# A dense two-layer stage: input forms made earlier, the mixer's output product in one pass, and the first group's input order changed

## The chip, the core and the metric

One core of one Trainium2 chip runs the whole program in one launch. The metric is the device time of that launch in microseconds; lower is better.

## What is computed

The reference has two blocks over 512 tokens of width 1024, in float32. The first (a gated linear recurrence and a mixture of 32 experts) is not touched by the change. The second, `second_block`, has two layers, and each layer is three residual steps:

```
h = rmsnorm(x, g_ffn1); x = x + 0.5 * swiglu(h, w1_a, w3_a, w2_a)
h = rmsnorm(x, g_mix);  p = h @ w_in
x = x + (gate0 * y_f + gate1 * y_c + gate2 * y_p) @ w_o
h = rmsnorm(x, g_ffn2); x = x + 0.5 * swiglu(h, w1_b, w3_b, w2_b)
```

`swiglu(h)` is `(silu(h @ w1) * (h @ w3)) @ w2` with an inner width of 2816. `rmsnorm` divides each token by the root of the mean of its squares over all 1024 inputs. A last `rmsnorm` ends the program.

## The kernel before

**Numbers.** Every product is made in float32 by three matmuls (`mm3`, line 231): both operands are split into a rounded part (`hi`, written by ScalarE) and a remainder (`lo`, by VectorE), and hi x hi, hi x lo and lo x hi are added up in PSUM.

**Weights.** The class `Stream` loads weights as blocks of 128 x 2048 in a fixed order and cuts each in two halves of 128 x 1024. `_split` (lines 185 and 186) writes a half's rounded part `whi` on ScalarE and its remainder `wlo` on VectorE; there are 5 buffers of each. `advance(h)` splits until four halves lie ahead of half h. It is called in the program wherever a half has been used up, so its place in the text is its place in the queues of ScalarE and VectorE. Weights of `group` come in sets of seven halves with four sums among them; two sums are added by DMAs on POOL's queue (line 149, `accum_op`), two by VectorE (line 191). Ordinary loads stand on SP's queue (line 151). A block's slot is free again when its halves are split.

**X.** The residual is held as eight tiles X[0] to X[7] of 128 inputs by 512 tokens. Outputs are produced in the order JO = 0, 4, 1, 5, 2, 6, 3, 7.

**Feed-forward.** `ffn` (line 1526) goes through the inner width in three chunks CH (6, 8 and 8 tiles of 128). For each pair of inner tiles `group` (line 1458) computes w1 and w3 products with seven block products instead of eight (a Strassen-like scheme on 256-column halves); its inputs are sums and differences of pairs of X tiles, made by `forms(q)` (line 1339) from the tiles X[q] and X[q+4] scaled by the gain. `step(i, n, ps)` is one of the seven: 4 pairs q x 2 halves m x 3 matmuls of 256 columns, 24 in all, on the input form XS[n, q]. Step 0 uses n = 4 and step 1 uses n = 6. Between the steps ScalarE copies a PSUM bank on (`pv` is the copy of `pm`, line 1482), `after` runs leftovers of the group before and calls `advance`. In the very first chunk of the first layer (`std`) the plain scheme is used. There are 41 groups. The chunk's inner tiles then go through `out_part` (line 1405), whose order `out_order` starts the first two outputs without their last two inputs; each output, 24 matmuls of 512 columns with 8 inputs, is added to X[j] by `done` on VectorE (line 1571).

**What stands between two stages.** In a stage's last output product `done` also calls `nxt(j)`. Before a stage that uses `group` at once this is `prep_s` (line 1364): `gained` scales X[j] by the gain (ScalarE, 1337), `square` squares it (ScalarE, 1316) and adds the squares to `ssum` (POOL, 1319), and once both tiles of a pair are there `forms` is due. Both the sum and `forms` are not run at once but put in the list `late`, which the next `square` (after its own ScalarE instruction) or the end of the product empties by `flush`. In `forms` the lines that matter are 1346 (ScalarE, the rounded copy for n = 1 and 4), 1349 to 1351 (VectorE, sums), 1352, 1353 and 1356 (ScalarE, rounded copies), 1354 and 1357 to 1359 (VectorE, remainders). `rstd_1` (matmuls of `ssum` with ones, a root, Newton steps) and `rstd_2` (transposes into the row R) turn the sum of squares into the norm's factor; products in `group` are multiplied by R on their way out of PSUM. With `rstd` true, in the first group of a stage, `rstd_1` follows step 1 and `rstd_2` follows step 2.

**Mixer.** `mixer` (line 1576) makes eight gated tiles M[0] to M[7]. It does so in two halves of four; after each half `out_part2` (line 1432) adds that half's part of the product with w_o to all eight tiles of X, in a pipeline: the fourth input of an output is multiplied three outputs later (LAG2 = 3), and so the last three outputs all end within the last nine matmuls. Before the second half's product the mixer's buffers are closed and those of the next feed-forward (`open_ffn`, load slots `rawf` and `rawg` among them) opened. Three stages begin with a `group` on fresh forms: the second feed-forward of each layer, behind the mixer, and the first feed-forward of the second layer.

**Buffers.** Split inputs, forms, inner tiles and M share 45 slots `s` of 128 x 512; a feed-forward has 5 scratch tiles `t` and 2 wide ones `T`. PSUM has six banks `mm` and two `sv`.

Of the kernel before, what the change touches and what calls it, by code (L numbers as in the profile page):

```python
# [33 lines left out]
JO = (0, 4, 1, 5, 2, 6, 3, 7)  # L34
L2 = 2
NT_F = 5
LAG2 = 3
ALPHA = float(np.float32(2 ** 0.25))
LN_EPS = 1e-5
EPS = 1e-6  # L40
# [1202 lines left out]
def dense_phase(K):  # L1243
# [11 lines left out]
    def bank():  # L1255
        return pp.tile([128, 512], F32, name="mm", tag="mm", bufs=6)

    def sbank():

        return pp.tile([128, 512], F32, name="sv", tag="sv", bufs=2)  # L1260
# [49 lines left out]
    def flush():  # L1310
        while late:
            late.pop(0)()

    def square(k, E=nc.gpsimd):
        t = ssum if k == 0 else tmp()
        act(t, X[k], AF.Square)
        flush()
        if k:
            late.append(lambda: E.tensor_tensor(ssum, ssum, t, op=OP.add))

    def prep(k, g, sq=True):
        hi, lo = slot(), slot()
# [8 lines left out]
    def halves(t):  # L1331
        return t.rearrange("p (a b) -> p a b", a=2)
# [30 lines left out]

    def prep_s(k, g):
        gained(k, g)
        square(k)
        if k >= 4:
            late.insert(0, lambda: forms(k - 4))

    def rstd_1():  # L1370

# [33 lines left out]
    def out_part(x, done, tail=None):  # L1405

        nonlocal h
        n = 0
        ps = {}
        for j, ks in out_order(len(x)):  # L1410
            if tail and j == KD - 1:
                flush()
                tail(x, [tuple(t[:, q % 8 * 128:q % 8 * 128 + 128] for t in st.get(h + q // 8))
                         for q in range(n, n + len(x))])
                n += len(x)
                break
            if j not in ps:
                ps[j] = bank()
            for k in ks:
                w = st.get(h + n // 8)  # L1420
                sl = slice((n % 8) * 128, (n % 8 + 1) * 128)
                mm3(nc, ps[j], (w[0][:, sl], w[1][:, sl]), x[k], k == 0, k == len(x) - 1)
                n += 1
                if n % 8 == 0:
                    st.advance(h + n // 8 - 1)
            if ks[-1] == len(x) - 1:
                done(j, ps[j])
        flush()
        assert n % 8 == 0
        h += n // 8  # L1430

    def out_part2(x, done):

        nonlocal h
        ps = {}
        n = 0
        for i in range(KD + LAG2):
            for j, ks in ((i, range(3)), (i - LAG2, (3,))):
                if not 0 <= j < KD:
                    continue  # L1440
                if ks[0] == 0:
                    ps[j] = bank()
                for k in ks:
                    w = st.get(h + n // 8)
                    sl = slice((n % 8) * 128, (n % 8 + 1) * 128)
                    mm3(nc, ps[j], (w[0][:, sl], w[1][:, sl]), x[k], k == 0, k == 3)
                    n += 1
                    if n % 8 == 0 and n < 4 * KD:
                        st.advance(h + n // 8 - 1)
                if ks[0] == 3:  # L1450
                    done(JO[j], ps[j])
        flush()
        st.advance(h + 3)
        h += n // 8

    RB = [R[:, None, i * 256:(i + 1) * 256].to_broadcast([128, 2, 256]) for i in range(2)]
# [1 line left out]
    def group(hid, todo, rstd):  # L1458
# [1 line left out]

        nonlocal h

        def step(i, n, ps, first=False):
            w = st.get(h + i)
            for q in range(4):
                for m in range(2):
                    sl = slice(m * 512 + q * 128, m * 512 + (q + 1) * 128)
                    mm3(nc, ps[:, m * 256:(m + 1) * 256], (w[0][:, sl], w[1][:, sl]), XS[n, q],
                        first and q == 0 and m == 0, q == 3, True)

        def after(i, *fs):
            for f in todo[i:i + 1] + list(fs):
                f()
            st.advance(h + i)
# [1 line left out]
        def tile():  # L1476
            return wide().rearrange("p (t m b) -> p t m b", t=2, m=2)

        pm = bank()
        step(0, 4, pm, True)  # L1480
        pv = sbank()
        act(pv, pm, AF.Copy)
        after(0)
        pz = bank()
        step(1, 6, pz, True)
        zs = tmp()
        act(zs, pz, AF.Copy)
        if rstd:
            rstd_1()
        after(1)  # L1490
        step(2, 0, pv)
        pw = sbank()
        act(pw, pv, AF.Copy)
        after(2)
        if rstd:
            pr, = rstd_2(0)
            act(R, pr, AF.Copy)
        step(3, 2, pm)
        a = tile()
        after(3, lambda: STT(a[:, 1], halves(pm), -1.0, RB[1], op0=OP.mult, op1=OP.mult))  # L1500
        step(4, 1, pw)
        vs = tmp()
        act(vs, pw, AF.Copy)
# [72 lines left out]
    def mixer(l, nxt):  # L1576
# [105 lines left out]
        for g in range(4):  # L1682
# [7 lines left out]
            TT(f[:, 1:256], p1[:, 1:256], q[:, 1:256], op=OP.subtract)  # L1690
            TT(f[:, 511:256:-1], p1[:, 1:256], q[:, 1:256], op=OP.add)
            FT.append(hilo(f))
        for half in range(2):
            M = []
            for j in range(4 * half, 4 * half + 4):
                g = j // 2
                gc, gf = gate(), gate()
                w = st.get(h)
                py, pf, pq = sbank(), bank(), sbank()
                chunk(w, BC, py)  # L1700
                mm3(nc, pf, (w[0][:, 512:640], w[1][:, 512:640]), FT[g], True, True)
                mm3(nc, pq, (w[0][:, 640:768], w[1][:, 640:768]), PL[g], True, True)
                st.advance(h)
                h += 1
                TT(gc, gc, py, op=OP.mult)
                TT(gf, gf, pf, op=OP.mult)
                TT(gc, gc, gf, op=OP.add)
                gp = gate()
                STT(gp, pq, vc("pscale", KD * l + j), gp, op0=OP.mult, op1=OP.mult)
                TT(gc, gc, gp, op=OP.add)  # L1710
                M.append(hilo(gc))
                if j % 2 == 0 and g < 3:
                    PL[g + 1] = pool(g + 1)

            def done(j, ps):
                TT(X[j], ps, X[j], op=OP.add)
                if half == 1:
                    nxt(j)
            if half == 1:
                close()  # L1720
                open_ffn(2 * l + 1)
            out_part2(M, done)

    def last(k):
        square(k)
# [95 lines left out]
def layout(I):  # L1821
# [70 lines left out]
    for l in range(L2):  # L1892
# [27 lines left out]
        for j in range(KD):  # L1920
            g, r = divmod(j, 2)
            sl = slice(128 * r, 128 * r + 128)
            misc = np.zeros((128, 8, 128), f)
            misc[:, 0:4] = tco[j]
            misc[:, 4] = W["w_fourier"][g][:, sl]
            misc[:, 5] = W["w_pool"][g][:, sl]
            hv += [gates[1, j], gates[0, j], misc, gates[2, j]]
            if r == 0 and g < 3:
                hv.append(pool[g + 1])
            if j % 4 == 3:  # L1930
                t2 = tiles(W["w_o"])[:, :, j - 3:j + 1].transpose(0, 2, 1, 3)
                t2 = np.stack([t2[JO[jj], k] for i in range(KD + LAG2) for jj, ks in ((i, range(3)), (i - LAG2, (3,)))
                               if 0 <= jj < KD for k in ks])
                hv += list(t2.reshape(-1, 8, 128, 128).transpose(0, 2, 1, 3))
        put(np.stack([np.ascontiguousarray(v).reshape(128, HB) for v in hv]))
        ffn("b")
    t = np.arange(S)
# [33 lines left out]
```

## Time and profile before

| | us |
|---|---|
| median of three runs | 3007.39 |
| lowest and highest | 3005.86, 3008.48 |
| the profiled execution, its time | 3006.73 |
| the profiled execution, its span | 3004.9 |

The span runs from the first to the last instruction of the profiled execution; its time is measured around it. Times in the trace are microseconds from the span's start. The second block takes the time from about 863 us on. A matmul's record is longer than the distance to the next one, since matmuls overlap; what counts is where one starts and how long TensorE was idle before it ("idle before <- who ended it").

### The profile page before, as it was taken

Reading aid. Unit: us, or ns where it says so; the run is one execution under the profiler, and the core shown is the slowest. Engines: PE = TensorE matmul, PEld = TensorE weight load, DVE = VectorE, ACT = ScalarE, POOL = GpSimd, SP = SyncE. Lnnn points to the kernel's source line nnn. Section 1 sums busy time; section 2 is a strip of 40 time slices with the busy share of each in tenths; the row PEclk is TensorE's granted clock in tenths of the full one; section 3 lists DMA queues with packets and bytes.
Section 4 is the critical chain, followed back from the end, with each engine's and each line's share of the span. In section 5 each row is a group of like instructions: output and inputs, shape, how many; then the busy total and the mean of one; then the engine's idle time right before and its main releaser. Section 6 shows DMA issues by size and latency. Waiting matters only on the chain.

```text
span 3004.9 us, 40511 instructions
## 1 busy us (share of the span) xinstructions
PE 2891.4 (96%) x16306; PEld 2428.4 (81%) x16306; DVE 2090.3 (70%) x2550; ACT 1535.8 (51%) x2046; POOL 347.5 (12%) x317
## 2 busy tenths in 40 slices
PE   9997999999899999999989999899999999989998
PEld 7875666667568989878869989799898788789997
DVE  7688898888976857455567657677575555676674
ACT  4756888888754535333235435545353332354442
POOL 0025222220500000000010000100001000100002
PEclk9998999999999999999999999999999999989999
DMA  5374999999833554222235555455542232345551
GB/s 193 121 280 154 342 357 343 372 371 377 331 122 112 170 143 137 98 85 98 98 98 160 149 147 155 121 153 156 146 148 98 72 105 104 112 121 162 160 145 66
DMA packets 93103, 517.11 MB, mean 172 GB/s; under 512 B 10652, under 2 KB 21276, under 8 KB 40048
## 3 DMA queue, kind: packets, MB, share of 16 engines
q1 hardware_dynamic: 76944, 463.28, 42.1%
q0 software_dynamic: 14880, 50.16, 8.9%
q8 instruction: 129, 2.11, 0.3%
q10 hardware_dynamic: 1088, 1.05, 0.1%
q14 instruction: 62, 0.51, 0.1%
HBM read 504.28 MB, written 14.16 MB: 173 GB/s over the span
## 4 chain that ended last, share of the span: by engine, by line
PE 73%; DVE 6%; ACT 3%; issue 1%; DMA 0%; POOL 0%; POOLq 0%; DVEq 0%; ACTq 0%
PE mm L235 15%; PE mm L234 15%; PE mm L236 15%; PE sv L234 7%; PE sv L235 7%; PE sv L236 7%; DVE wlo L186 3%; PE y L936 2%; ACT whi L185 2%; PE h L901 1%; PE h L900 1%; PE ht L914 1%; PE gat L871 0%; DVE s L1354 0%; DVE t L1351 0%
## 5 line engine op out<-in xcount | busy, mean ns | idle before, releaser
L234 PE MATMUL mm<-s,whi 128*128 128x512 f32 (+1 forms) x2464 | 867.3, 352 | 29.9 <-ACT s L1346 27.2
L235 PE MATMUL mm<-s,whi 128*128 128x512 f32 (+1 forms) x2464 | 866.4, 352 | 11.2 <-DVE s L1354 11.2
L236 PE MATMUL mm<-s,wlo 128*128 128x512 f32 (+1 forms) x2464 | 863.8, 351 | 0.0
L186 DVE TENSOR_TENSOR wlo<-raw,whi 128x1024 fp32r<-128x1024 f32 x505 | 623.7, 1244 | 272.0 <-ACT whi L185 271.9
L185 ACT ACTIVATE whi<-raw 128x1024 fp32r<-128x1024 f32 x507 | 526.1, 1051 | 200.1 <-PE mm L235 142.4
L234 PEld LDWEIGHTS mm<-s,whi 128*128 128x128 f32 x2464 | 468.5, 190 | 97.3 <-ACT s L1346 29.2
L235 PEld LDWEIGHTS mm<-s,whi 128*128 128x128 f32 x2464 | 468.8, 190 | 78.9 <-DVE s L1354 13.5
L236 PEld LDWEIGHTS mm<-s,wlo 128*128 128x128 f32 x2464 | 469.1, 190 | 65.0
L234 PE MATMUL sv<-s,whi 128*128 128x256 f32 (+1 forms) x1504 | 446.5, 297 | 0.0
L235 PE MATMUL sv<-s,whi 128*128 128x256 f32 (+1 forms) x1504 | 446.3, 297 | 0.0
L236 PE MATMUL sv<-s,wlo 128*128 128x256 f32 (+1 forms) x1504 | 444.7, 296 | 0.0
L236 PEld LDWEIGHTS sv<-s,wlo 128*128 128x128 f32 x1504 | 283.8, 189 | 8.5
L235 PEld LDWEIGHTS sv<-s,whi 128*128 128x128 f32 x1504 | 283.4, 188 | 8.4
L234 PEld LDWEIGHTS sv<-s,whi 128*128 128x128 f32 x1504 | 283.1, 188 | 8.4
L186 DVE TENSOR_TENSOR wlo<-rawb,whi 128x1024 fp32r<-128x1024 f32 x162 | 200.0, 1276 | 22.0 <-ACT whi L185 18.4
L901 PE MATMUL h<-wlo,xt 128*64 128x512 f32 x512 | 195.5, 402 | 6.5 <-DVE wlo L186 5.6
L900 PE MATMUL h<-whi,xt 128*128 128x512 f32 x448 | 180.8, 403 | 6.1 <-PEq L1112 5.2
L186 DVE TENSOR_TENSOR wlo<-rawf,whi 128x1024 fp32r<-128x1024 f32 x110 | 134.3, 1221 | 70.2 <-ACT whi L185 70.2
L1571 DVE SCALAR_TENSOR_TENSOR X<-mm,X 128x512 f32<-128x512 f32 x95 | 65.3, 688 | 161.3 <-PE mm L236 161.3
L185 ACT ACTIVATE whi<-rawb 128x1024 fp32r<-128x1024 f32 x162 | 163.4, 1055 | 0.1
L936 PE MATMUL y<-whi,hd 128*64 128x512 f32 x512 | 160.6, 394 | 2.8 <-ACT whi L185 1.5
L186 DVE TENSOR_TENSOR wlo<-rawa,whi 128x1024 fp32r<-128x1024 f32 x114 | 139.0, 1254 | 20.8 <-ACT whi L185 19.2
(398 smaller groups left out, 3815.2 us busy)
## 6 DMA issues: line engine op xcount, KB each, us to landing
raw<-in_wblocks SPq DMA_DIRECT2D x229, 1024.0 KB, 4.8
rawb<-in_wblocks SPq DMA_DIRECT2D x81, 1024.0 KB, 6.7
rawa<-in_wblocks SPq DMA_DIRECT2D x57, 1024.0 KB, 6.5
rawf<-in_wblocks SPq DMA_DIRECT2D x36, 1024.0 KB, 5.2
rawg<-in_wblocks SPq DMA_DIRECT2D x41, 512.0 KB, 3.6
rawg<-in_wblocks POOLq DMA_DIRECT2D x41, 512.0 KB, 6.9
raw<-in_wblocks POOLq DMA_DIRECT2D x22, 512.0 KB, 5.5
rawf<-in_wblocks POOLq DMA_DIRECT2D x19, 512.0 KB, 5.5
```

Source lines behind the costliest of these rows:

```text
L185: self.nc.scalar.activation(hi, src, AF.Copy)
L186: f = lambda E=self.nc.vector: E.tensor_tensor(lo, src, hi, op=OP.subtract)
L234: nc.tensor.matmul(ps, wh, xh, start=first, stop=False, skip_group_check=skip)
L235: nc.tensor.matmul(ps, wh, xl, start=False, stop=False, skip_group_check=skip)
L236: nc.tensor.matmul(ps, wl, xh, start=False, stop=last, skip_group_check=skip)
L900: nc.tensor.matmul(ps, x, w[0][:, sl], start=k == 0, stop=False)
L901: nc.tensor.matmul(ps[:64], x[:, 0:64], w[1][:, sl], start=False, stop=False)
L914: nc.tensor.matmul(ps[:, 256 * i + 64 * f:256 * i + 64 * f + 64], HS[i][:, 128 * f:128 * f + 128], K["i2"], start=True, stop=True)
L936: nc.tensor.matmul(ps[i][:64], hd[:, f, v:v + 64], w[wv][:, sl], start=f == 0 and n == 0, stop=f == 3 and n == 2)
L1571: STT(X[j], ps, 0.5, X[j], op0=OP.mult, op1=OP.add)
```

## The change

- `square` puts a sum on POOL into the queue directly and defers only a sum on VectorE. `prep_s` runs `forms(k - 4)` directly after `gained`, ahead of the square; the sum of the last tile, k = 7, goes to VectorE.
- `out_part` calls `advance` after `done` where a half ends with an output's last input.
- `out_part2` goes. The mixer makes all eight M, then one `out_part` over eight inputs; the order of the w_o weights in `layout` follows.
- In `group` with `rstd` true, pairs q = 0 to 2 of steps 0 and 1 come first, then q = 3 of step 0, the copy to `pv`, and q = 3 of step 1. `rstd_1` follows step 2 and `rstd_2` step 3. In every group the multiplication of `pm` by R (line 1500) comes after the `advance` of step 3 and not before it.

```diff
--- before.py
+++ after.py
@@ -34,7 +34,6 @@
 JO = (0, 4, 1, 5, 2, 6, 3, 7)
 L2 = 2
 NT_F = 5
-LAG2 = 3
 ALPHA = float(np.float32(2 ** 0.25))
 LN_EPS = 1e-5
 EPS = 1e-6
@@ -1315,8 +1314,11 @@
         t = ssum if k == 0 else tmp()
         act(t, X[k], AF.Square)
         flush()
-        if k:
-            late.append(lambda: E.tensor_tensor(ssum, ssum, t, op=OP.add))
+        f = lambda: E.tensor_tensor(ssum, ssum, t, op=OP.add)
+        if k and E is V:
+            late.append(f)
+        elif k:
+            f()
 
     def prep(k, g, sq=True):
         hi, lo = slot(), slot()
@@ -1363,9 +1365,9 @@
 
     def prep_s(k, g):
         gained(k, g)
-        square(k)
         if k >= 4:
-            late.insert(0, lambda: forms(k - 4))
+            forms(k - 4)
+        square(k, V if k == KD - 1 else nc.gpsimd)
 
     def rstd_1():
 
@@ -1421,48 +1423,26 @@
                 sl = slice((n % 8) * 128, (n % 8 + 1) * 128)
                 mm3(nc, ps[j], (w[0][:, sl], w[1][:, sl]), x[k], k == 0, k == len(x) - 1)
                 n += 1
-                if n % 8 == 0:
+                if n % 8 == 0 and k < len(x) - 1:
                     st.advance(h + n // 8 - 1)
             if ks[-1] == len(x) - 1:
                 done(j, ps[j])
+                if n % 8 == 0:
+                    st.advance(h + n // 8 - 1)
         flush()
         assert n % 8 == 0
         h += n // 8
 
-    def out_part2(x, done):
+    RB = [R[:, None, i * 256:(i + 1) * 256].to_broadcast([128, 2, 256]) for i in range(2)]
+
+    def group(hid, todo, rstd):
+
 
         nonlocal h
-        ps = {}
-        n = 0
-        for i in range(KD + LAG2):
-            for j, ks in ((i, range(3)), (i - LAG2, (3,))):
-                if not 0 <= j < KD:
-                    continue
-                if ks[0] == 0:
-                    ps[j] = bank()
-                for k in ks:
-                    w = st.get(h + n // 8)
-                    sl = slice((n % 8) * 128, (n % 8 + 1) * 128)
-                    mm3(nc, ps[j], (w[0][:, sl], w[1][:, sl]), x[k], k == 0, k == 3)
-                    n += 1
-                    if n % 8 == 0 and n < 4 * KD:
-                        st.advance(h + n // 8 - 1)
-                if ks[0] == 3:
-                    done(JO[j], ps[j])
-        flush()
-        st.advance(h + 3)
-        h += n // 8
-
-    RB = [R[:, None, i * 256:(i + 1) * 256].to_broadcast([128, 2, 256]) for i in range(2)]
-
-    def group(hid, todo, rstd):
-
-
-        nonlocal h
-
-        def step(i, n, ps, first=False):
+
+        def step(i, n, ps, first=False, qs=range(4)):
             w = st.get(h + i)
-            for q in range(4):
+            for q in qs:
                 for m in range(2):
                     sl = slice(m * 512 + q * 128, m * 512 + (q + 1) * 128)
                     mm3(nc, ps[:, m * 256:(m + 1) * 256], (w[0][:, sl], w[1][:, sl]), XS[n, q],
@@ -1476,28 +1456,32 @@
         def tile():
             return wide().rearrange("p (t m b) -> p t m b", t=2, m=2)
 
-        pm = bank()
-        step(0, 4, pm, True)
+        pm, pz = bank(), bank()
+        if rstd:
+
+            step(0, 4, pm, True, range(3))
+            step(1, 6, pz, True, range(3))
+        step(0, 4, pm, not rstd, range(3 if rstd else 0, 4))
         pv = sbank()
         act(pv, pm, AF.Copy)
         after(0)
-        pz = bank()
-        step(1, 6, pz, True)
+        step(1, 6, pz, not rstd, range(3 if rstd else 0, 4))
         zs = tmp()
         act(zs, pz, AF.Copy)
+        after(1)
+        step(2, 0, pv)
         if rstd:
             rstd_1()
-        after(1)
-        step(2, 0, pv)
         pw = sbank()
         act(pw, pv, AF.Copy)
         after(2)
+        step(3, 2, pm)
         if rstd:
             pr, = rstd_2(0)
             act(R, pr, AF.Copy)
-        step(3, 2, pm)
+        after(3)
         a = tile()
-        after(3, lambda: STT(a[:, 1], halves(pm), -1.0, RB[1], op0=OP.mult, op1=OP.mult))
+        STT(a[:, 1], halves(pm), -1.0, RB[1], op0=OP.mult, op1=OP.mult)
         step(4, 1, pw)
         vs = tmp()
         act(vs, pw, AF.Copy)
@@ -1690,36 +1674,33 @@
             TT(f[:, 1:256], p1[:, 1:256], q[:, 1:256], op=OP.subtract)
             TT(f[:, 511:256:-1], p1[:, 1:256], q[:, 1:256], op=OP.add)
             FT.append(hilo(f))
-        for half in range(2):
-            M = []
-            for j in range(4 * half, 4 * half + 4):
-                g = j // 2
-                gc, gf = gate(), gate()
-                w = st.get(h)
-                py, pf, pq = sbank(), bank(), sbank()
-                chunk(w, BC, py)
-                mm3(nc, pf, (w[0][:, 512:640], w[1][:, 512:640]), FT[g], True, True)
-                mm3(nc, pq, (w[0][:, 640:768], w[1][:, 640:768]), PL[g], True, True)
-                st.advance(h)
-                h += 1
-                TT(gc, gc, py, op=OP.mult)
-                TT(gf, gf, pf, op=OP.mult)
-                TT(gc, gc, gf, op=OP.add)
-                gp = gate()
-                STT(gp, pq, vc("pscale", KD * l + j), gp, op0=OP.mult, op1=OP.mult)
-                TT(gc, gc, gp, op=OP.add)
-                M.append(hilo(gc))
-                if j % 2 == 0 and g < 3:
-                    PL[g + 1] = pool(g + 1)
-
-            def done(j, ps):
-                TT(X[j], ps, X[j], op=OP.add)
-                if half == 1:
-                    nxt(j)
-            if half == 1:
-                close()
-                open_ffn(2 * l + 1)
-            out_part2(M, done)
+        M = []
+        for j in range(KD):
+            g = j // 2
+            gc, gf = gate(), gate()
+            w = st.get(h)
+            py, pf, pq = sbank(), bank(), sbank()
+            chunk(w, BC, py)
+            mm3(nc, pf, (w[0][:, 512:640], w[1][:, 512:640]), FT[g], True, True)
+            mm3(nc, pq, (w[0][:, 640:768], w[1][:, 640:768]), PL[g], True, True)
+            st.advance(h)
+            h += 1
+            TT(gc, gc, py, op=OP.mult)
+            TT(gf, gf, pf, op=OP.mult)
+            TT(gc, gc, gf, op=OP.add)
+            gp = gate()
+            STT(gp, pq, vc("pscale", KD * l + j), gp, op0=OP.mult, op1=OP.mult)
+            TT(gc, gc, gp, op=OP.add)
+            M.append(hilo(gc))
+            if j % 2 == 0 and g < 3:
+                PL[g + 1] = pool(g + 1)
+
+        def done(j, ps):
+            TT(X[j], ps, X[j], op=OP.add)
+            nxt(j)
+        close()
+        open_ffn(2 * l + 1)
+        out_part(M, done)
 
     def last(k):
         square(k)
@@ -1927,11 +1908,9 @@
             hv += [gates[1, j], gates[0, j], misc, gates[2, j]]
             if r == 0 and g < 3:
                 hv.append(pool[g + 1])
-            if j % 4 == 3:
-                t2 = tiles(W["w_o"])[:, :, j - 3:j + 1].transpose(0, 2, 1, 3)
-                t2 = np.stack([t2[JO[jj], k] for i in range(KD + LAG2) for jj, ks in ((i, range(3)), (i - LAG2, (3,)))
-                               if 0 <= jj < KD for k in ks])
-                hv += list(t2.reshape(-1, 8, 128, 128).transpose(0, 2, 1, 3))
+        t2 = tiles(W["w_o"])
+        hv += list(np.stack([t2[j, :, k] for j, ks in out_order(KD) for k in ks])
+                   .reshape(-1, 8, 128, 128).transpose(0, 2, 1, 3))
         put(np.stack([np.ascontiguousarray(v).reshape(128, HB) for v in hv]))
         ffn("b")
     t = np.arange(S)
```

## Rows read from the trace of the kernel before

**Rows 1.** The page, engine shares: busy us, share of the span, instructions.

```profile
PE 2891.4 (96%) x16306; PEld 2428.4 (81%) x16306; DVE 2090.3 (70%) x2550; ACT 1535.8 (51%) x2046; POOL 347.5 (12%) x317
```

**Rows 2.** TensorE's waits over the whole run: us in total, times, longest.

```profile
PE mm L234 <- ACT s L1346: 27.2, 8, 4.5
...
PE mm L235 <- DVE s L1354: 11.2, 8, 1.5
...
PE mm L235 <- DVE wlo L186: 0.8, 1, 0.8
```

**Rows 3.** Timeline of TensorE, 1926 to 1937: start, length, idle before.

```profile
1926.80 0.39 PE L234 MATMUL mm<-s,whi 128*128 128x256 f32 x1 [0.52 <-ACT s L1346]
1928.25 0.39 PE L235 MATMUL mm<-s,whi 128*128 128x256 f32 x1 [1.06 <-DVE s L1354]
...
1928.59 0.28 PE L234 MATMUL mm<-s,whi 128*128 128x256 f32 x1
1928.71 0.29 PE L235 MATMUL mm<-s,whi 128*128 128x256 f32 x1
...
1933.65 0.58 PE L234 MATMUL mm<-s,whi 128*128 128x256 f32 x1 [4.54 <-ACT s L1346]
1935.76 0.58 PE L235 MATMUL mm<-s,whi 128*128 128x256 f32 x1 [1.53 <-DVE s L1354]
1936.14 0.41 PE L236 MATMUL mm<-s,wlo 128*128 128x256 f32 x1
1936.35 0.41 PE L234 MATMUL mm<-s,whi 128*128 128x256 f32 x1
```

**Rows 4.** Windows: length, busy (instructions) of PE, PEld, DVE, ACT, POOL; granted clock; DMA.

```profile
1564.40:1584.80 20.40, 8.55 (x31) 7.09 (x32) 19.14 (x27) 12.21 (x22) 6.15 (x5) 0.50 0.01 1
1929.60:1939.80 10.20, 4.62 (x20) 4.33 (x21) 8.12 (x13) 5.20 (x9) 2.98 (x3) 0.50 0.66 165
2625.90:2649.80 23.90, 10.73 (x41) 9.26 (x42) 20.91 (x29) 13.55 (x24) 6.97 (x5) 0.50 0.09 27
```

**Rows 5.** Timeline of VectorE, 1920 to 1938, same columns as rows 3.

```profile
1921.49 1.54 DVE L186 TENSOR_TENSOR wlo<-raw,whi 128x1024 fp32r<-128x1024 f32 x1 [2.26 <-ACT whi L185]
1923.07 1.23 DVE L191 TENSOR_TENSOR raw<-raw 128x1024 f32<-128x1024 f32 x1
...
1929.66 0.41 DVE L1359 TENSOR_TENSOR s<-t,s 128x256 fp32r<-128x256 f32 x1
...
1931.13 0.67 DVE L1571 SCALAR_TENSOR_TENSOR X<-mm,X 128x512 f32<-128x512 f32 x1
...
1933.27 1.50 DVE L1350 TENSOR_TENSOR t<-T 128x256 f32<-128x256 f32 x1
...
1935.03 0.68 DVE L1354 SCALAR_TENSOR_TENSOR s<-T,s 128x512 fp32r<-128x512 f32 x1
...
1937.17 0.41 DVE L1359 TENSOR_TENSOR s<-t,s 128x256 fp32r<-128x256 f32 x1
```

**Rows 6.** Timeline of VectorE after the first mixer's output product.

```profile
1561.47 1.28 DVE L1716 TENSOR_TENSOR X<-mm,X 128x512 f32<-128x512 f32 x2
```

**Rows 7.** Timeline of ScalarE, 1930 to 1938.

```profile
1931.84 0.72 ACT L1337 ACTIVATE T<-X,vec 128x512 f32<-128x512 f32 x1 [1.91 <-DVE X L1571]
1932.46 0.61 ACT L1316 ACTIVATE t<-X 128x512 f32<-128x512 f32 x1
...
1936.08 0.42 ACT L1356 ACTIVATE s<-t 128x256 fp32r<-128x256 f32 x1 [0.31 <-DVE t L1355]
1937.23 0.58 ACT L1482 ACTIVATE sv<-mm 128x512 f32<-128x512 f32 x1 [0.74 <-PE mm L236]
1937.72 1.05 ACT L185 ACTIVATE whi<-raw 128x1024 fp32r<-128x1024 f32 x1
```

**Rows 8.** Timeline of POOL, 1900 to 1958.

```profile
1933.22 1.27 POOL L1319 TENSOR_TENSOR ssum<-ssum,t 128x512 f32<-128x512 f32 x1 [5.57 <-ACT t L1316]
```

**Rows 9.** Line 1319: instruction, count, ns min/median/max, first and last start.

```profile
L1319 DVE TENSOR_TENSOR ssum<-ssum,t x7: 684/692/695, 873.6 to 878.4; 128x512 f32<-128x512 f32 x7
```

## Prediction

> **What bounds the kernel now.** Read first the page's engine shares [rows 1]: TensorE is busy 96% of the span, so a change pays only where TensorE waits, or runs at its lower clock. The waits of TensorE come next [rows 2]: in the dense part there is one large cause, the input forms that `forms` makes. 27.2 us are spent on `s` of line 1346 (ScalarE's rounded copy of the negated tile), 11.2 us on `s` of line 1354 (VectorE's remainder), 8 times each; together 38.4 us. They lie in the first `group` of the three stages that begin on `forms`: after each mixer's output product, and after the first layer's second feed-forward. The splitting of weights (`wlo`) makes TensorE wait 0.8 us there, once [rows 2].
>
> The timeline of TensorE shows the middle place [rows 3]. The output product ends at E = 1926.28 (1926.80 less its 0.52 idle), and four waits follow, 0.52, 1.06, 4.54 and 1.53: 7.65 us. The two mixers share the other 30.8, 15.4 each. Matmuls of 256 columns start 0.12 us apart before the long wait and 0.21 after it [rows 3]. The windows show why [rows 4]: for 20.4, 10.2 and 23.9 us around the three places the granted clock is 0.50, so 1.2 GHz and not 2.4, after the engine had been mostly idle. In those windows 92 matmuls ran (31 + 20 + 41).
>
> Why the forms are late is on VectorE's timeline [rows 5]. Tile X[6] is done two outputs before the end, but `forms(2)` is held in `late` until X[3] has been squared: its last remainder starts at 1929.66. A weight split follows, and only at 1931.13 comes the update of X[7], whose matmuls ended at E: 4.85 us late. The mixer is worse [rows 6]: by the lag of 3 its last tiles finish together, their updates come in pairs, the first at 1561.47, and three `forms` stand in a row.
>
> **The change, part by part.** *Mixer's product in one go.* The multiplications are the same, 8 outputs by 8 inputs, three matmuls each. 8 of 16 updates of X per mixer go, 16 x 0.64 us [rows 6], on VectorE where nothing waits for it: nothing on the path. With the lag gone the last outputs end 24 matmuls apart, 5.6 us at 0.23 us each (512 columns, twice the 0.12 of 256), as in the feed-forward. The last gate's M[7] needs some six VectorE and ScalarE steps of 0.7 us, 4.4 us, after its matmuls; TensorE has 36 matmuls, 8.4 us, before it needs it. Cost nothing; without that cover 4.4 us per mixer. Slots: 16 of M and 28 of forms, 44 of 45, so no new wait if the count is right (a rival). The feed-forward's load slots open 22 us earlier, so its loads on SP's and POOL's queues go out sooner: more lead, no time.
>
> *Forms at once, last sum on VectorE.* VectorE step by step, from X[6] ending at E - 11.2. Update and forms take 5.4 us (1931.13 to 1937.58, less the 1.09 us by which line 1350 was held, 1.50 against 0.41 for that shape [rows 5]): E - 5.7. The next split, 1.5 us where it meets POOL's sum [rows 5]: E - 4.2. Update of X[3], 0.7: E - 3.5. ScalarE's scaling, square and half split, 2.3 us [rows 7], since the advance now stands behind `done`: E - 1.2. Remainder 1.5: E + 0.3. The half-sum of line 191, 1.2 [rows 5]: E + 1.5. So X[7] is updated at S = E + 1.5 where it is E + 4.85 now; with VectorE free, S = E + 0.1.
>
> *Last inputs last.* TensorE has 36 matmuls of the first three pairs, 4.3 us at 0.12, until E + 4.1. Then it needs the remainder of 1354, at S + 3.5 (1935.03 + 0.68 - 1931.13 - 1.09): E + 5.0, wait 0.9. Six matmuls: E + 5.7; the next remainder comes 0.9 after the first: wait 0.2. Six more: E + 6.6. Now a wait that is new: step 2 adds onto `pv`, ScalarE's copy of `pm`, and six matmuls (0.7 us) cover it, not 24 (2.9 us). Queued ahead of the copy on ScalarE are the fourth form (line 1356; 1936.08 + 0.42 less 1931.13 and 1.09: S + 4.3), the square and a weight split; it takes 0.58 itself [rows 7]: S + 6.4, so E + 7.9, wait 1.3. In all S - E + 0.9 per stage: 2.4 us, 1.0 with VectorE free.
>
> The sum for k = 7 costs VectorE 0.69 [rows 9], after the split; it is done before `rstd_1`, which now follows step 2: nothing. The chain from `rstd_1` to R keeps one step, 2.9 us, between its two TensorE parts: nothing; uncovered it would be some 2.5 us a stage. POOL's loads queued behind the sum of 1933.22 [rows 8] no longer wait for the last square; that eases the second group's loads.
>
> *Advance after done, STT after advance.* 14 output products split their weights behind the update of X, 0.7 us later, and in a stage's last third behind forms, by up to 4.8 us. A split is four halves ahead of its use, 4 x 5.6 = 22 us: nothing. The 41 updates of line 1500 now stand behind a split and at times a half-sum, 2.4 us; their bank is taken again three groups later, their tile used two steps later: nothing.
>
> **POOL's lock.** Line 1350 took 1.50 us, begun 0.05 us after a sum on POOL of 1.27 us [rows 5, 8], against 0.41 for that shape: VectorE stood until POOL had ended. The split at 1921.49, which met only the tail of a sum, took 1.54 [rows 5]. Two sums (k = 6 and 3) still fall between X[6] and X[7]; 0.3 us for each is in the steps above, and I add 0.6, since the first now meets the last remainder. In full they would hold VectorE 2.6 us, not 0.6: S = E + 3.5, 4.4 us of waits a stage. The Trainium skill, "SBUF — State Buffer", section "SBUF: two separate sides", says that VectorE with two inputs in SBUF and GpSimd take a shared port pair as an exclusive lock, the loser blocked for a whole instruction. By that page the second rival below is the time to expect.
>
> **The sum.** Gone: waits, 38.4 us; loss by the clock, 92 x (0.21 - 0.12), 8.3 us. New: waits, 3 x (2.4 + 0.6) = 9.0 us, between 3.0 (VectorE free) and 13.2 (sums in full); a clock that falls again, between 0 and 3 x 1.8 (the 20 matmuls of the shortest window), taken at 2.0, near the low end because the waits are short, though the fall of rows 4's second window began before the 4.54 us had passed. Gain 38.4 + 8.3 - 9.0 - 2.0 = 35.7, from 44 to 28. The profiled execution took 3006.73 us (span 3004.9); less 35.7 that is 2971.0. The median of the runs shown, 3007.39, is 0.66 higher, so 2972; the ends are 2964 and 2979.
>
> **Rivals.** *The last pair stays late* (0.14): VectorE falls further behind, and each stage keeps the 7.65 us of today's middle one and its low clock. Gain 38.4 - 23.0 + 8.3 - 5.4 = 18: 2989. For it: three long VectorE items between X[6] and X[7]; against: by the steps above they cost a lag of only 1.5 us.
>
> *POOL's sums hold VectorE in full* (0.10): 13.2 us of waits, clock fallen in all three: gain 28, 2979.
>
> *The mixer's slots run short* (0.06): if a 46th were wanted, the last forms would wait for M, read until E. Both mixer stages stay as they are, and the gain is the middle stage's 7.65 + 1.8 - 3.0 = 6.5: 3001. Against: the count of 44.
>
> *Slower, the lead of the weights* (0.05): place, the 14 products; with the split behind the update every block's remainder is 0.6 us later. If the lead of four halves were used up, TensorE would pay at 14 x 8 blocks, 67 us, less the gain of 36: 3038. It decides from a delay above 22 us; against it stand the 0.8 us on `wlo` today [rows 2] and 4.8 us as the longest delay.
>
> *The waits come back elsewhere in full* (0.03): 3007. The forecast keeps 0.62.
>
> **How the numbers follow.** A change within 0.2%, 6 us, can't be told from none here. Faster by more: 0.62 + 0.14 + 0.10 and half of the slot case, 0.89; within: 0.03 + 0.03; slower: 0.05. The range runs from 2962 (the best bounds and some run-to-run spread) to 2989, the first rival: with the forecast, POOL's case and most of the first rival it holds 0.82.
>
> **What would show it.** TensorE's waits on lines 1346 and 1354 fall from 38 us to a few; a new wait stands three times, step 2 of the first groups on the copy `pv`, some 1.3 us each. VectorE updates X[7] 1.5 to 2 us behind the last matmul. The granted clock is near 1 at the three places, with short falls at most. TensorE's matmul counts are unchanged. The prediction is wrong if X[7] is updated over 4 us late, if TensorE waits for `whi` or `wlo` at a stage's start, or if the mixer's gates show new waits.

## The result, and the profile after

The changed kernel takes 2979.66 us (median of 4 runs, 2979.14 to 2981.56) against 3007.93 of the kernel before (4 runs): a ratio of 0.9907, 95% interval 0.989 to 0.9924. It is faster by 28.3 us, where 36 were forecast; 2979.66 lies inside the range, near the time of the second rival, in which the sums on POOL hold VectorE in full (2979). The experiments below show that these sums are one of two things that made VectorE late, and the trace shows that most of the lag arose ahead of X[6], where the forecast had none.

TensorE's waits in the profile of the changed kernel (us in total, times, longest), the two that answer to [rows 2] and the splits of weights; line 1348 is what was 1346, line 1356 what was 1354:

```profile
PE mm L233 <- ACT s L1348: 12.9, 3, 4.5
...
PE mm L234 <- DVE s L1356: 2.3, 3, 0.8
...
PE mm L234 <- DVE wlo L185: 0.8, 1, 0.8
```

38.4 us in 16 waits have become 15.2 in six, two at each of the three places. The wait on `wlo` lies ahead of 200 us, in the first block, in both kernels; in the second block TensorE waits for no split. The spans differ by 27.0 us (3004.9 and 2977.9); the waits make 23.2 of it. The rest is the clock. The windows at 1.2 GHz, against [rows 4] (length; busy us and instructions of PE, PEld, DVE, ACT, POOL; granted clock; DMA):

```profile
1569.40:1576.20 6.80, 4.22 (x16) 3.63 (x17) 5.60 (x11) 5.95 (x10) 0.00 (x0) 0.50 0.00 0
1921.00:1927.80 6.80, 4.52 (x17) 3.93 (x18) 5.60 (x11) 6.25 (x10) 0.00 (x0) 0.50 0.74 136
2617.30:2624.10 6.80, 4.91 (x19) 4.32 (x20) 5.95 (x11) 6.33 (x11) 0.00 (x0) 0.50 0.00 0
```

They last 20.4 us and not 54.5, and 52 matmuls ran in them and not 92: 40 x 0.09 = 3.6 us. With the waits that is 26.8 of the 27.0. So close a fit is in part chance: the second block's first matmul starts at 864.80 here and at 863.30 before, 1.5 us later behind work that the change leaves alone.

The middle place on TensorE's timeline, against [rows 3] (start, length, idle before):

```profile
1913.72 0.40 PE L235 MATMUL mm<-s,wlo 128*128 128x512 f32 x1
1913.96 0.28 PE L233 MATMUL mm<-s,whi 128*128 128x256 f32 x1
...
1922.50 0.58 PE L233 MATMUL mm<-s,whi 128*128 128x256 f32 x1 [4.12 <-ACT s L1348]
1923.84 0.58 PE L234 MATMUL mm<-s,whi 128*128 128x256 f32 x1 [0.76 <-DVE s L1356]
```

The product's last matmul ends at 1914.12, and 36 matmuls of 256 columns follow at once, as the new order has it. Then TensorE waits 4.12 us for the last pair's first form. VectorE says why, against [rows 5]:

```profile
1907.23 0.68 DVE L1555 SCALAR_TENSOR_TENSOR X<-mm,X 128x512 f32<-128x512 f32 x1
...
1914.70 0.68 DVE L1555 SCALAR_TENSOR_TENSOR X<-mm,X 128x512 f32<-128x512 f32 x1
1917.64 1.53 DVE L185 TENSOR_TENSOR wlo<-raw,whi 128x1024 fp32r<-128x1024 f32 x1 [2.26 <-ACT whi L184]
1919.21 1.23 DVE L190 TENSOR_TENSOR raw<-raw 128x1024 f32<-128x1024 f32 x1
1920.35 0.68 DVE L1555 SCALAR_TENSOR_TENSOR X<-mm,X 128x512 f32<-128x512 f32 x1
1921.82 0.69 DVE L1351 TENSOR_TENSOR t<-T 128x512 f32<-128x512 f32 x1 [0.79 <-ACT T L1339]
...
1923.10 0.68 DVE L1356 SCALAR_TENSOR_TENSOR s<-T,s 128x512 fp32r<-128x512 f32 x1
```

The first line is the update of X[6], which TensorE had done at 1902.92: VectorE is 4.3 us late already. X[3], done 24 matmuls before the end, at 1908.5, is updated at 1914.70; X[7] at 1920.35, 6.23 us behind the product, not the 2.1 of the forecast (1.5, and 0.6 for POOL). From there on the forecast's steps fit: the first remainder (1923.10 + 0.68) stands 3.43 us behind the update, 3.5 were reckoned. In the kernel before, X[7] was updated 6.3 us behind this product, so at this place it comes no earlier; the wait is shorter because 36 matmuls, 4.3 us, now run first.

### The profile page after: what moved, and what is told of

It is laid out like the page before. It is cut to its first block, busy times and chain, and to the rows that moved or that the text cites. A ratio compares the mean times of both kernels' runs of the same rounds, so it can differ in the third digit from the quotient of the medians.

```text
span 2977.9 us, 40475 instructions
## 1 busy us (share of the span) xinstructions
PE 2886.6 (97%) x16306; PEld 2420.3 (81%) x16306; DVE 2073.7 (70%) x2537; ACT 1538.3 (52%) x2046; POOL 346.0 (12%) x314
## 3 DMA queue, kind: packets, MB, share of 16 engines
q8 instruction: 129, 2.11, 0.3%
## 4 chain that ended last, share of the span: by engine, by line
PE 73%; DVE 6%; ACT 3%; issue 2%; DMA 0%; POOL 0%; POOLq 0%; DVEq 0%; ACTq 0%
PE mm L234 15%; PE mm L233 15%; PE mm L235 15%; PE sv L233 7%; PE sv L235 7%; PE sv L234 7%; DVE wlo L185 3%; PE y L935 2%; PE h L900 2%; ACT whi L184 2%; PE h L899 1%; PE ht L913 1%; PE gat L870 1%; ACT T L1339 0%; ACT t L1315 0%
## 5 line engine op out<-in xcount | busy, mean ns | idle before, releaser
L185 DVE TENSOR_TENSOR wlo<-rawf,whi 128x1024 fp32r<-128x1024 f32 x114 | 140.3, 1231 | 57.9 <-ACT whi L184 57.9
```

Source lines behind the costliest of these rows:

```text
L185: f = lambda E=self.nc.vector: E.tensor_tensor(lo, src, hi, op=OP.subtract)
```

## What holds VectorE back: experiments

Two theories. **A**: the sums of squares on POOL hold VectorE whenever the two overlap, in all outputs from X[4] on, and the lag is carried along. **B**: in every output VectorE waits for ScalarE, which scales and squares the tile before it splits the next half (2.26 us idle ahead of 1917.64 above).

**No sums.** `square` returns before the sum in `prep_s`; seven of eight tiles' squares are left out of the norm in three stages.

```diff
+        if E is None:
+            return
...
-        square(k, V if k == KD - 1 else nc.gpsimd)
+        square(k, None)
```

> The changed kernel without the seven sums of squares per stage in prep_s (the norm then rests on one tile's squares; three stages leave this work out). In the changed kernel the update of X[7] starts 6.2 to 6.6 us behind the output product's last matmul, not 1.5 to 2.1 as forecast. Theory A: POOL's sums hold VectorE in passing, some 4 us between X[5] and X[7]. Then without them X[7] is updated 2 to 2.5 us behind, TensorE's wait per stage falls from 5.1 to about 3 us, and the time is 2968 to 2973. Theory B: VectorE is late because in every output it waits for ScalarE's scaling and square ahead of the half's split. Then X[7] stays over 5 us late, and the time is 2976 to 2980.

Measured: 2965.36 us, ratio 0.9856 (0.984 to 0.9872). X[7] is updated 2.2, 2.9 and 2.2 us behind the product in the three stages. A holds, and its time was reckoned too high. TensorE's waits are now the ones that the forecast named, `pv` among them:

```profile
PE mm L234 <- DVE s L1358: 2.9, 3, 1.0
PE sv L233 <- ACT sv L1468: 2.8, 3, 0.9
...
PE mm L233 <- ACT s L1350: 0.8, 1, 0.8
```

0.95 us a stage for the remainder (0.9 forecast), 0.94 for the copy `pv` (1.3 forecast). In the changed kernel itself the copy is not waited for: TensorE is late, and at the lower clock, when it gets there.

**Sums on VectorE.** The same question without leaving work out: each sum stands in `late` behind the next tile's update or forms.

```diff
-        square(k, V if k == KD - 1 else nc.gpsimd)
+        square(k, V)
```

> The changed kernel with all seven sums of squares of a stage on VectorE, each run behind the next tile's update or forms, where VectorE waits for ScalarE anyway (2.26 us before the split of an open pair, 0.42 before that of a closed one); all work is done. Theory A (the cost is POOL's hold on VectorE, not the sums themselves): X[7] is updated 2 to 3.5 us behind the product, TensorE waits 2 to 3.5 us a stage, 2966 to 2971. If VectorE has no room for another 4.8 us a stage: X[7] 6 us late or more, 2977 to 2984.

Measured: 2967.48 us, ratio 0.9864 (0.9848 to 0.9881); X[7] 2.3, 3.1 and 2.4 us behind. So it is POOL's place, not the additions, that costs. The groups of VectorE in one stretch (1536 to 1570, the last outputs of the first mixer's product and what follows) show the hold; first the changed kernel, then this one (count, busy us, mean ns, idle before):

```profile
L185 DVE TENSOR_TENSOR wlo<-raw,whi 128x1024 fp32r<-128x1024 f32 x4 | 6.7, 1672 | 3.5 <-ACT whi L184 3.5
L1699 DVE TENSOR_TENSOR X<-mm,X 128x512 f32<-128x512 f32 x6 | 4.1, 680 | 0.0
L1356 DVE SCALAR_TENSOR_TENSOR s<-T,s 128x512 fp32r<-128x512 f32 x2 | 3.2, 1624 | 0.0
L185 DVE TENSOR_TENSOR wlo<-rawf,whi 128x1024 fp32r<-128x1024 f32 x2 | 2.8, 1376 | 4.5 <-ACT whi L184 4.5
L1351 DVE TENSOR_TENSOR t<-T 128x512 f32<-128x512 f32 x2 | 2.1, 1071 | 1.6 <-ACT T L1339 1.6
```

```profile
L185 DVE TENSOR_TENSOR wlo<-raw,whi 128x1024 fp32r<-128x1024 f32 x4 | 4.9, 1220 | 2.1 <-ACT whi L184 2.1
L1699 DVE TENSOR_TENSOR X<-mm,X 128x512 f32<-128x512 f32 x6 | 4.1, 684 | 0.1
...
L185 DVE TENSOR_TENSOR wlo<-rawf,whi 128x1024 fp32r<-128x1024 f32 x2 | 2.4, 1224 | 3.3 <-ACT whi L184 3.3
L1351 DVE TENSOR_TENSOR t<-T 128x512 f32<-128x512 f32 x3 | 2.1, 693 | 2.4 <-ACT T L1339 2.4
L1356 DVE SCALAR_TENSOR_TENSOR s<-T,s 128x512 fp32r<-128x512 f32 x3 | 2.1, 685 | 0.0
```

The splits take 1672 and 1376 ns instead of 1220 and 1224, lines 1356 and 1351 take 1624 and 1071 instead of 685 and 693: 4 x 0.45 + 2 x 0.15 + 2 x 0.94 + 2 x 0.38 = 4.7 us in this stage, for six sums. The forecast priced only the two that it put between X[6] and X[7], at 1.2 in all (0.3 for each, and 0.6). The update of X takes 680 and 684 ns, but in the changed kernel none meets a sum; in a kernel further down some do.

One hold came in a way the forecast had not looked for. VectorE, then POOL, in the changed kernel ahead of the middle place:

```profile
1894.21 1.81 DVE L1352 TENSOR_TENSOR t<-T 128x256 f32<-128x256 f32 x1
1895.94 0.41 DVE L1353 TENSOR_TENSOR t<-T 128x256 f32<-128x256 f32 x1
```

```profile
1893.52 0.88 POOL L148 DMA_DIRECT2D raw<-in_wblocks  x1 [6.48 <-DMA raw<-in_wblocks]
1894.11 1.61 POOL L1317 TENSOR_TENSOR ssum<-ssum,t 128x512 f32<-128x512 f32 x1
1898.41 1.57 POOL L1317 TENSOR_TENSOR ssum<-ssum,t 128x512 f32<-128x512 f32 x1 [2.68 <-ACT t L1315]
```

The sum of X[1] stands in POOL's queue behind a load that waited 6.48 us for the transfer it adds to. So it ran not after its own square but in the middle of the next tile's forms, and line 1352 took 1.81 us instead of 0.42.

**Twice the work on POOL.** A second addition, t plus t in place, behind each of the six sums.

```diff
+            if twice:
+                E.tensor_tensor(t, t, t, op=OP.add)
...
-        square(k, V if k == KD - 1 else nc.gpsimd)
+        square(k, V if k == KD - 1 else nc.gpsimd, True)
```

> The changed kernel with a second addition on POOL behind each of the six sums of a stage that it holds (t plus t in place, not used by anything), so twice the time in which POOL reads and writes the same memory as VectorE. Theory A: what holds VectorE about doubles, X[7] comes another 3 to 5 us later, and the time is 2988 to 3000. If the sums on POOL cost by something else (the wait of VectorE or TensorE for ssum, the scratch tiles): X[7] as in the changed kernel within 1 us, 2979 to 2982.

Measured: 2990.44 us, ratio 0.9945 (0.993 to 0.996); X[7] 10.8, 9.1 and 10.7 us behind, 2.9 to 4.4 more than in the changed kernel. A holds from this side too. Splits come so late here that TensorE waits for them as well (5.0 us in three waits).

**The split first.** For the first tile of a pair, whose scaled form nobody needs yet, the next half's split stands ahead of the scaling; sums as in the changed kernel.

```diff
-    def prep_s(k, g):
+    def prep_s(k, g, split=None):
+        if split and k < 4:
+            split()
         gained(k, g)
...
```

The rest of the edit hands the `advance` of `out_part` down to this place.

> The changed kernel with sums on POOL as it has them, but for the first tile of a pair (j below 4) the next half's split stands between the update of X and the scaling and square, so VectorE need not wait 2.3 us for ScalarE. Theory B (that wait makes the lag): X[7] comes 3 to 5 us earlier, 2968 to 2973. Theory A alone: 1 to 2 us earlier at most, since the sums still hold VectorE, 2975 to 2980.

Measured: 2966.26 us, ratio 0.9863 (0.9847 to 0.988); X[7] 2.4, 3.5 and 1.9 us behind. That is a little better than B's range: B holds as well, and A alone would not give it. VectorE in the middle stage of this kernel, then POOL:

```profile
1906.54 1.83 DVE L185 TENSOR_TENSOR wlo<-raw,whi 128x1024 fp32r<-128x1024 f32 x1 [0.41 <-ACT whi L184]
1908.29 0.68 DVE L1560 SCALAR_TENSOR_TENSOR X<-mm,X 128x512 f32<-128x512 f32 x1
1908.89 1.21 DVE L185 TENSOR_TENSOR wlo<-raw,whi 128x1024 fp32r<-128x1024 f32 x1
1910.13 1.23 DVE L190 TENSOR_TENSOR raw<-raw 128x1024 f32<-128x1024 f32 x1
1911.27 0.68 DVE L1560 SCALAR_TENSOR_TENSOR X<-mm,X 128x512 f32<-128x512 f32 x1
```

```profile
1910.39 2.11 POOL L1317 TENSOR_TENSOR ssum<-ssum,t 128x512 f32<-128x512 f32 x1 [3.10 <-ACT t L1315]
```

The split at 1908.89 follows the update of X[3] without a gap. The one at 1906.54 is still held (1.83 us). Over the stage the six sums hold VectorE's instructions for 3.6 us, against 3.8 in the changed kernel's middle stage, so the gain is not POOL's. The update of X[7] at 1911.27 meets a sum and takes 0.68 us all the same.

From the update of X[6] to that of X[7] VectorE takes 13.1 us in the changed kernel's middle stage, 12.3 with the sums on VectorE and 10.5 with the split first; TensorE makes the two outputs in 11.2. So either repair, less POOL or less waiting for ScalarE, takes most of the lag away: the period of two outputs was over-full by both, and neither is the cause alone.

**Both.** The two edits above together.

> Sums on VectorE and the split first for the first tile of a pair, together. If A holds and B adds a part: X[7] within 2 us of the product, 2962 to 2967, ahead of the kernel with the sums on VectorE alone. If the sums now fill the time that the split had waited: the same as that kernel within 2 us.

Measured: 2960.39 us, ratio 0.9843 (0.9827 to 0.986), below both ranges, and 2959.36, 0.9839 (0.9825 to 0.9852), when it ran again beside the next kernel. X[7] is updated 0.04 us behind the product in both mixer stages and 1.8 us in the middle one; TensorE waits 0.6, 1.8 and 0.6 us. By the times alone the intervals of this kernel and of each single repair still touch; the lag tells them apart.

What is left in the middle stage goes with something that neither theory has. Between X[2] and X[6] a half-sum of weights waits for its load:

```profile
1895.87 1.23 DVE L190 TENSOR_TENSOR raw<-raw 128x1024 f32<-128x1024 f32 x1 [3.02 <-DMA raw<-in_wblocks]
```

The half-sums of the mixer stages do not wait for a load, and there VectorE waits for TensorE at X[6] and X[7]. In the changed kernel this wait is 0.62 us. No run takes it away, so what it costs is not shown.

> The kernel with the sums on VectorE and the split first for the first tile of a pair, a second time, beside the next one: 2959 to 2962.

**And the last split behind the copy.** The wait that is left behind the mixers is the one for `pv`, whose copy stands behind a split on ScalarE. The edit comes on top of both.

```diff
-                    if n % 8 == 0:
+                    if n % 8 == 0 and not (early and j == KD - 1):
                         st.advance(h + n // 8 - 1)
```

> The same, and the advance of a stage's last half left to the first group, so that ScalarE's copy pv no longer stands behind a weight split of 1.05 us. If the copy's place on ScalarE is what step 2 waits for (0.58 us behind each mixer, 0.94 in the middle stage), those waits go and the time is 2957 to 2960; if the split that now comes later is missed by step 3, TensorE waits for it there and the time is 2960 to 2964.

Measured: 2957.03 us (2953.68 to 2958.71, 5 runs), ratio 0.9833 (0.9819 to 0.9846). No wait of TensorE is left behind the mixers; in the middle stage one is:

```profile
PE mm L234 <- DVE s L1356: 0.9, 1, 0.9
```

This version beats both kernels; against the version with both repairs its gain is 2.3 us at the median, what the copy's waits had been (0.58 + 0.94 + 0.59), with intervals that overlap. Single executions differ more than that: the first mixer's product ends at 1563.19 and 1558.69 in the profiles of these two kernels, which are the same up to there. A step of 2 us therefore rests on the waits of the traces.

## What each part of the change is worth: experiments

**The old order of steps 0 and 1.**

```diff
-            step(0, 4, pm, True, range(3))
-            step(1, 6, pz, True, range(3))
...
+        step(0, 4, pm, True)
...
+        step(1, 6, pz, True)
```

> The changed kernel with steps 0 and 1 of each stage's first group in the old order (all four pairs of step 0, then step 1). The forms of the last pair come as late as before, but 18 matmuls less are done by then: 2.1 us per stage, up to 3.8 where they run at the lower clock. Theories A and B alike: 2986 to 2991. Rival (the order is worth nothing, since the copy pv is now uncovered): 2979 to 2981.

Measured: 2986.59 us, ratio 0.9923 (0.9906 to 0.9939). TensorE waits 7.6, 7.4 and 8.5 us in the three stages and not 5.3, 4.9 and 5.0. X[7] is 0.2 and 0.4 us later in the first two and 1.5 in the third. So the order is worth some 5 to 7 us, by 18 matmuls a stage, as reckoned; by the times alone the interval still touches that of the changed kernel.

**Forms and sums in `late` again.**

```diff
-        if k >= 4:
-            forms(k - 4)
-        square(k, V if k == KD - 1 else nc.gpsimd)
+        square(k)
+        if k >= 4:
+            late.insert(0, lambda: forms(k - 4))
```

`square` puts every sum into `late` again, as in the kernel before.

> The changed kernel with forms and sums in the list late again (the last sum on POOL too). The forms of the last pair then stand behind the square and behind a weight split, some 3.5 us later, and forms(2) behind X[3]: 2990 to 2998 under A and B. If VectorE's queue is so full that the order within it doesn't matter: 2979 to 2983.

Measured: 2986.01 us, ratio 0.9921 (0.9905 to 0.9938), outside both ranges. X[3] is updated 2.0 to 2.3 us ahead of the product's end and not 0.6 to 1.0 behind it, since forms(2) now follows it; X[7] comes 5.9 to 6.2 us behind, as in the changed kernel, with the same items ahead of it in another order. Only the last pair's own chain is longer: behind the update of X[7] the first form is begun 1.3 us later and the first remainder 2.9, not 3.5. TensorE waits 7.2, 7.5 and 7.1 us. The early forms are worth some 5 to 6 us and not 10 to 18.

**The mixer's product in two halves again.**

> The changed kernel with the mixer's output product in two halves with the lag of 3 again. In the two mixer stages the last four tiles end within 2.1 us, so two to three forms stand in a row behind the product: 7 us more wait and 1 to 2 us more at the lower clock per mixer, 2994 to 3002; the middle stage is unchanged. Rival (the one-pass product is worth nothing by itself): 2979 to 2982.

The edit puts back `out_part2`, the loop over halves and the order of the w_o weights. Measured: 2998.73 us, ratio 0.9962 (0.9948 to 0.9976). VectorE behind the first mixer, where the product ends at 1561.69:

```profile
1563.49 0.68 DVE L1725 TENSOR_TENSOR X<-mm,X 128x512 f32<-128x512 f32 x1
...
1568.71 1.29 DVE L1725 TENSOR_TENSOR X<-mm,X 128x512 f32<-128x512 f32 x2
...
1575.70 1.28 DVE L1725 TENSOR_TENSOR X<-mm,X 128x512 f32<-128x512 f32 x2
```

The last updates come in pairs again, as in [rows 6], up to 14.6 us behind. TensorE waits 11.1 and 11.4 us in the mixer stages. The one pass is the largest part of the change, 18 or 19 of its 28 us. The middle stage, which this edit leaves alone, has X[7] 1.1 us earlier than in the changed kernel: a difference of 1 us in one stage of one profile shows nothing.

**The advance ahead of done again.**

```diff
-                if n % 8 == 0 and k < len(x) - 1:
+                if n % 8 == 0:
                     st.advance(h + n // 8 - 1)
             if ks[-1] == len(x) - 1:
                 done(j, ps[j])
-                if n % 8 == 0:
-                    st.advance(h + n // 8 - 1)
```

> The changed kernel with the advance of a half ahead of done again, in all output products. Split, half-sum and update then stand in the old order on VectorE; a period holds the same items, so X[7] moves by 1 us at most: 2977 to 2983. If putting the update ahead of the split was what made X[7] late (part of B): 2970 to 2975; if it had been a main part of the gain: 2986 to 2992.

Measured: 2982.7 us, ratio 0.9917 (0.9901 to 0.9934). X[7] comes 8.1 to 8.5 us behind, 1.5 to 2.2 later and not 1 at most; TensorE waits 6.8 to 7.1 us a stage. The placement is worth 3 us by the medians, which the intervals don't tell from none.

All runs, with X[7]'s update behind the product's end and TensorE's waits at the first group, each for the three stages:

| kernel | us | X[7] behind | waits |
|---|---|---|---|
| before | 3007.93 | 16.1, 6.3, 16.1 | 15.4, 7.7, 15.4 |
| changed | 2979.66 | 6.6, 6.2, 6.4 | 5.3, 4.9, 5.0 |
| no sums | 2965.36 | 2.2, 2.9, 2.2 | 1.9, 2.7, 1.9 |
| sums on VectorE | 2967.48 | 2.3, 3.1, 2.4 | 2.1, 2.9, 2.2 |
| POOL's work twice | 2990.44 | 10.8, 9.1, 10.7 | 9.1, 7.5, 7.9 |
| split first | 2966.26 | 2.4, 3.5, 1.9 | 2.1, 3.2, 1.9 |
| sums on VectorE, split first | 2960.39 | 0.0, 1.8, 0.0 | 0.6, 1.8, 0.6 |
| and the last split behind the copy | 2957.03 | 0.0, 1.8, 0.0 | 0, 0.9, 0 |
| old order of steps | 2986.59 | 6.8, 6.6, 7.8 | 7.6, 7.4, 8.5 |
| forms in late | 2986.01 | 5.9, 6.2, 5.9 | 7.2, 7.5, 7.1 |
| mixer in halves | 2998.73 | 14.6, 5.1, 14.7 | 11.1, 4.3, 11.4 |
| advance ahead | 2982.7 | 8.1, 8.5, 8.2 | 6.8, 7.1, 6.8 |

The four parts undone one at a time cost 7, 6, 19 and 3 us by the medians, 35 in all against the 28 of the whole. But the runs were made at different times: measured against the kernel before in the same round it is 5.5, 4.9, 17.7 and 3.3, 31 in all, and with some 5 us of interval on each that is not told from 28. The waits in the traces do say that the parts lean on each other: undone one at a time they bring back 8.3, 6.6, 11.6 and 5.5 us, 32 in all, where the whole change took away 23.2.

## Why the prediction was right, and where a step failed

**Right.** The place: the waits of TensorE on the forms at three places, and the clock that falls with them. The way of each part: the one-pass product takes the row of three forms away; 36 matmuls cover the start of the last pair's chain; the mixer's gates show no new wait, nor do slots or the splits of weights. The sign and the range. The waits removed and the clock's old loss, read from the trace of the kernel before, fit what was measured (26.8 of 27.0 us, with the new losses taken off).

**The step that failed** is where VectorE's reckoning starts: at X[6] "ending at E - 11.2", as if VectorE were on time there. It is 3.9, 4.3 and 3.4 us late at X[6] in the three stages. From X[6] to X[7] the steps were sized well: 13.9, 13.1 and 14.1 us, where the forecast has 12.7, or 13.3 with its 0.6 for POOL. POOL's hold shows the same: "0.3 us for each is in the steps above, and I add 0.6" makes 1.2 us between X[6] and X[7], and it is 1.7, 0.9 and 1.8 there; the 3.1, 2.9 and 2.6 us of hold ahead of X[6] were put at nothing. So X[7] came 6.2 to 6.6 us behind the product, and TensorE's new waits are 15.2 us where "9.0" stood; even the high end, 13.2, was too low. The clock's loss, "taken at 2.0", is 52 x 0.09 = 4.7 us: it fell once at each place, for 6.8 us. The two make up the 8.9 us by which the sum of 35.7 exceeds 26.8.

**By its own signs** the forecast failed on how late VectorE is. It said that it is wrong if X[7] is updated over 4 us late, and that is what happened; the wait on `pv` that it named does not stand in the changed kernel. The time lies in the range because the range took in two rivals in which VectorE falls further behind, held at 0.14 and 0.10, and something of each is in the trace. As in the first, X[7] comes as late as before in the middle stage; the 7.65 us of wait that this rival keeps did not come, since the new order of steps 0 and 1 covers part of it (with the old order it is 7.4 to 8.5 us a stage). As in the second, POOL's sums hold VectorE.

**A smaller slip.** The forecast put the end of the middle product at 1926.28, the first wait. It ended at 1924.86: twelve matmuls of the first two pairs ran behind it. X[7] had been 6.3 us late there, not 4.85. And the 0.8 us on `wlo`, which the forecast places among the waits of the dense part and sets against the rival on the lead of the weights, lies in the first block; the lead was better than it reckoned.

**The Trainium skill's rule** on the port that VectorE and GpSimd share ("SBUF — State Buffer", "SBUF: two separate sides"), the forecast's second rival, agrees with the trace in kind: line 1352, begun while a sum ran, ended 0.3 us after it, and the update that reads PSUM was not held where it met a sum (at 1911.27 in the kernel with the split first). It does not cost VectorE the sums' full length: 4.7 us in a stage with six sums of 1.3 to 1.6 us, for an instruction often begins late in a sum, as the split at 1917.64 does, 0.84 us into one. That rival's time, 2979, was right, and its place only partly: it had the two sums behind X[6] alone.

## What to carry to other kernels

A lag on an engine that keeps up on average is carried from output to output, so work out a queue from the last point where it is seen idle and not from the last output but two. Where a tight VectorE stretch runs beside additions on POOL, price the additions by what they do to VectorE's own instructions: moving them to VectorE cost less than leaving them. In a queue that must be served in order, put first what the next stage waits for, and what only refills a lead of several blocks (here the split of the next half, or its place before a copy) where the engine would be waiting anyway.

## What was not expected of the hardware

POOL pays too: its sums took 1.29 us alone and mostly 1.57 to 1.64 us where they met VectorE's instructions; the one above that began 0.26 us into a half-sum took 2.11 us. VectorE was held once even where it had begun first: in the first mixer's product line 1356 began at 1543.17, the sum at 1543.57, and line 1356 took 2.57 us and not 0.69; POOL's issue of a load, begun at 1542.97, was under way then. And the clock fell after short waits at times: for 3.4 us in the middle stage of the kernels with sums left out or on VectorE, where TensorE had waited 0.8 to 1.0 us three times. The kernel with both repairs had such a fall there in one profile and none in the other, with the same two waits of 0.9 us, and the kernel with the split first had none behind waits of 1.4, 0.9 and 0.9 us.
